# Two PSUM tiles in place of one, order edges at the context rows and key rotation, chain buffers turned by one, weight sums three steps later

## The chip, the cores and the metric

One Trainium2 chip, one core of it. The metric is the device time of one execution in microseconds, taken as the median of several runs. The engines are TensorE (PE, matmuls and transposes into PSUM), VectorE (DVE), ScalarE (ACT), GpSimd (POOL) and SyncE (SP); the last two mostly issue transfers (DMAs).

## The reference

One layer of a diffusion transformer block over 512 tokens of width 2048, with 256 context tokens. In float32:

```
h  = modulate(rmsnorm(x),   shift,   scale)          # from c @ w_ada
hc = modulate(rmsnorm(ctx), shift_c, scale_c)
kc, vc = keys and values of hc;  p = h @ w_in        # 2048 x 9216
q = rope(rmsnorm(q)) * d**-0.5 ;  k = rope(rmsnorm(k))
attn = softmax(q [k, kc]^T) [v, vc]                  # 12 query heads, 4 key/value heads of 128, 768 keys
y_a = (attn * silu(z_a)) @ w_proj_a
y_b = (fourier_mix(u_b) * silu(z_b)) @ w_proj_b
y   = (sigmoid(g_a) * y_a + sigmoid(g_b) * y_b) @ w_out
out = rmsnorm(x + gate * y) * final_g
```

## The kernel before

**Matmuls.** Every float32 factor is split in two halves, high and low (`split_from`, L174-177: ACT copies the high half, L176, and DVE subtracts it to get the low one, L177). `mm3` (L325-329) makes each product of three matmuls: high by high (L327), high by low (L328), low by high (L329). PSUM has eight banks of 512 float32 columns.

**Products of a group.** The large products are done in groups with seven products each (P1, Q5, P2, Q6, P7, Q3, Q4; a Strassen-like scheme), in place of eight. Each takes a form of the activations (A11, Z5, S2, S3, S4, A12, A22) by weights that are sums or differences of blocks. Groups 0 to 7 are the input projection (three of queries and gates, two of gates, group 5, `KV`, of keys and values together with the context's, two of gates); groups 10 and 11 are the projection of the attention branch; groups 8 and 9 the output projection. `Group.steps` runs the pieces of one product: `get` hands out the split weights of a piece, `mm` does its matmuls into an accumulator of two banks, and at a product's end DVE (L860) or ACT (L863, L868) empties the accumulator.

**The weight stream.** `stream_product` (L378) lists the pieces; `start_load` (L199) starts their loads on SP as buffers come free; `split_piece` splits them. Four of the seven weights are stages of a running sum in four chain buffers `chain[0..3]` (R in the profile), one for each piece: stage 0 is loaded, and after each split a POOL transfer adds the next block to the buffer (L280). `left[pc]` is 1 while a chain buffer is in use; a stage 0 isn't loaded before it is 0. `last_split` holds the instructions of the last split; `tc.issue_after` adds an order edge, so that what is emitted in it is issued behind the instruction named.

**Who sets the order.** The program is written as one sequence. A framework puts each engine's instructions in an order of its own within the dependencies, and places the semaphore waits: an instruction that writes a tile waits for those that read it before, and the other way round. Engines run their queues in order.

**Context and keys.** `context_row` (L1070) scales rows of the context by a modulation (four multiplications on DVE, L1077), makes the forms in one buffer `cparts` and stores them (`cf_d`). `rotations` (L931, L935) folds the norm's gain into the rotary tables, once for queries and once, before product Q5 of group 5, for keys, after `load_rotations` has loaded them.

**Attention.** PSUM is one tile of eight banks, `whole_psum` (L1200-1202). `banks[0]` is its first six banks and `banks[1]` the last two. The six are cut into four stretches of 768 columns, `wide[0..3]`, one and a half banks each. The loop over 48 steps (L1425-1479, one for each head and block of 128 queries) emits in each step:

- `scores(i)`: six matmuls into one of wide[0..2] in turn; maximum on DVE (L1272); exponential and sum on ACT (L1274).
- `values`, each second step: 18 matmuls of 256 columns for the half before, and two transposes of gates, into the last bank (`b1`); read by ACT (L1315) and DVE (L1316).
- `turn(i-1)`: six transposes of the probabilities (L1290) into wide[3], split into `pth` (L176) and `ptl` (L177).
- `fill`: groups of three matmuls of the other branch's projection into bank 6 (`fill_acc`), emptied by DVE at L1238.
- three times in the whole loop `get_keys`: six transposes and a split for the next keys; eleven times `turn_queries` into `b1`.
- `weight_sum`: six sums of three weight blocks, by a load (L1415), an accumulating load (L1416) and a store (L1417) on POOL, at the steps 10 to 27.

**Behind the attention** `pair` hands out pairs of banks from the same `banks`: 0 to 5 as accumulators, 6 and 7 for the transposes of merged rows (`turn_merged`, L1404), which ACT copies out (L1408). `branch_done` multiplies an accumulator by its gate (L1388), `out_done` by a row of gates (L1615).

## Time and profile before

| what | us |
|---|---|
| median of 3 runs | 1311.36 |
| lowest and highest run | 1309.23, 1312.31 |
| the profiled execution | 1312.46 |
| its span (first to last instruction) | 1310.7 |

The profile's page names each engine's busy time and share of the span, and groups of instructions by line. A timeline row holds start, length, engine, line, operation, what it writes and reads, the shape and, in brackets, how long the engine stood idle before it and what ended that. A row of groups holds the count, the busy time and the mean of one in ns, then the idle time before them. A window's row holds the busy time of PE, its weight loads, DVE, ACT and POOL with the counts of instructions, then the granted clock of PE, the share of the DMA engines and GB/s. Matmuls are pipelined: the time from one start to the next is the cadence, and it is shorter than the length in the row.

### The profile page before, as it was taken

Reading aid. Unit: us, or ns where it says so; the run is one execution under the profiler, and the core shown is the slowest. Engines: PE = TensorE matmul, PEld = TensorE weight load, DVE = VectorE, ACT = ScalarE, POOL = GpSimd, SP = SyncE. Lnnn points to the kernel's source line nnn. Section 1 sums busy time; section 2 is a strip of 40 time slices with the busy share of each in tenths; the row PEclk is TensorE's granted clock in tenths of the full one; section 3 lists DMA queues with packets and bytes.
Section 4 is the critical chain, followed back from the end, with each engine's and each line's share of the span. In section 5 each row is a group of like instructions: output and inputs, shape, how many; then the busy total and the mean of one; then the engine's idle time right before and its main releaser. Section 6 shows DMA issues by size and latency. Waiting matters only on the chain.

```text
span 1310.7 us, 17551 instructions
## 1 busy us (share of the span) xinstructions
PE 1281.5 (98%) x6522; PEld 1046.7 (80%) x6522; DVE 995.5 (76%) x1295; ACT 685.8 (52%) x1079; POOL 183.3 (14%) x244
## 2 busy tenths in 40 slices
PE   6999999999999999999999999999999999999997
PEld 3577888888888887888888888888888888788885
DVE  5666899989688876757677766688898867787676
ACT  5222655555556544544254554666667646465554
POOL 0110011110202110011021020012100212221210
PEclk9999999999999999999999999999999999999999
DMA  9898487887899979986869888578852899998985
GB/s 381 330 374 349 177 244 188 240 249 244 213 291 263 260 245 276 297 215 175 262 210 285 273 212 260 195 228 264 270 163 81 236 253 246 242 205 231 219 204 171
DMA packets 103718, 318.54 MB, mean 243 GB/s; under 512 B 9808, under 2 KB 33104, under 8 KB 99280
## 3 DMA queue, kind: packets, MB, share of 16 engines
q0 software_dynamic: 30288, 123.75, 39.9%
q1 hardware_dynamic: 48720, 163.65, 35.2%
q10 hardware_dynamic: 24624, 30.02, 6.7%
q8 instruction: 51, 0.84, 0.2%
q14 instruction: 35, 0.29, 0.1%
HBM read 283.30 MB, written 34.09 MB: 242 GB/s over the span
## 4 chain that ended last, share of the span: by engine, by line
PE 73%; DMA 10%; DVE 9%; issue 3%; ACT 3%; SPq 0%; POOL 0%; ACTq 0%; DVEq 0%
PE banks L327 10%; PE banks L328 10%; PE banks L329 9%; PE x L329 6%; PE x L328 6%; PE x L327 6%; PE y L328 5%; PE y L329 5%; PE y L327 5%; DMA wr<-in_w_g 4%; DVE wlo L177 3%; PE pd L532 2%; PE banks L1290 2%; PE pb L327 2%; DVE s L177 2%
## 5 line engine op out<-in xcount | busy, mean ns | idle before, releaser
L176 ACT ACTIVATE whi<-R 128x1024 fp32r<-128x1024 f32 x138 | 145.4, 1060 | 131.6 <-PE banks L329 44.6
L177 DVE TENSOR_TENSOR wlo<-R,whi 128x1024 fp32r<-128x1024 f32 x138 | 167.7, 1222 | 55.3 <-ACT whi L176 53.0
L177 DVE TENSOR_TENSOR wlo<-wr,whi 128x1024 fp32r<-128x1024 f32 (+1 forms) x123 | 148.7, 1214 | 58.8 <-ACT whi L176 58.7
L176 ACT ACTIVATE whi<-wr 128x1024 fp32r<-128x1024 f32 (+1 forms) x123 | 128.9, 1053 | 119.3 <-PE y L329 36.6
L327 PE MATMUL banks<-whi,s 128*128 128x512 f32 x396 | 157.1, 397 | 2.1 <-DVE ev L860 1.5
L328 PE MATMUL banks<-wlo,s 128*128 128x512 f32 x396 | 155.2, 392 | 0.8 <-DVE wlo L177 0.8
L329 PE MATMUL banks<-whi,s 128*128 128x512 f32 x396 | 155.1, 392 | 0.0
L328 PE MATMUL x<-wlo,s 128*128 128x512 f32 x352 | 137.3, 390 | 2.9 <-DVE wlo L177 2.9
L327 PE MATMUL x<-whi,s 128*128 128x512 f32 x352 | 137.2, 390 | 0.0
L329 PE MATMUL x<-whi,s 128*128 128x512 f32 x352 | 137.0, 389 | 0.0
L328 PE MATMUL y<-wlo,s 128*128 128x512 f32 x316 | 123.1, 390 | 0.5 <-DVE wlo L177 0.5
L327 PE MATMUL y<-whi,s 128*128 128x512 f32 x316 | 123.0, 389 | 0.3 <-DVE cxe L1013 0.3
L329 PE MATMUL y<-whi,s 128*128 128x512 f32 x316 | 122.8, 389 | 0.0
L280 POOL DMA_DIRECT2D R<-in_w_g x64 | 56.0, 876 | 423.6 <-DVE wlo L177 241.1
L176 ACT ACTIVATE s<-wr 128x512 fp32r<-128x512 f32 (+2 forms) x93 | 60.7, 677 | 69.2 <-DMA wr<-cf_d 23.7
L327 PEld LDWEIGHTS banks<-whi,s 128*128 128x128 f32 x396 | 74.4, 188 | 17.9 <-ACT whi L176 2.2
L177 DVE TENSOR_TENSOR s<-wr,s 128x512 fp32r<-128x512 f32 (+2 forms) x93 | 67.0, 751 | 27.4 <-ACT s L176 26.6
L329 PEld LDWEIGHTS banks<-whi,s 128*128 128x128 f32 x396 | 74.4, 188 | 15.5
L328 PEld LDWEIGHTS banks<-wlo,s 128*128 128x128 f32 x396 | 74.5, 188 | 15.0 <-DVE wlo L177 1.2
L328 PEld LDWEIGHTS x<-wlo,s 128*128 128x128 f32 x352 | 66.1, 188 | 17.9 <-DVE wlo L177 4.2
L327 PEld LDWEIGHTS x<-whi,s 128*128 128x128 f32 x352 | 66.1, 188 | 13.7
L329 PEld LDWEIGHTS x<-whi,s 128*128 128x128 f32 x352 | 66.1, 188 | 13.6
(293 smaller groups left out, 2835.4 us busy)
## 6 DMA issues: line engine op xcount, KB each, us to landing
wr<-in_w_g SPq DMA_DIRECT2D x128, 512.0 KB, 5.2
R<-in_w_g POOLq DMA_DIRECT2D x64, 512.0 KB, 7.2
wa<-in_w_ss POOLq DMA_DIRECT2D x26, 1024.0 KB, 8.4
R<-in_w_g SPq DMA_DIRECT2D x32, 512.0 KB, 5.7
wr<-in_w_gate SPq DMA_DIRECT2D x32, 512.0 KB, 5.1
wr<-in_w_o SPq DMA_DIRECT2D x24, 512.0 KB, 7.7
R<-in_w_o POOLq DMA_DIRECT2D x24, 512.0 KB, 8.5
wr<-in_w_pab SPq DMA_DIRECT2D x20, 512.0 KB, 6.0
```

The costliest lines, as they stand in the source:

```text
L176: first = nc.scalar.activation(hi, src, ACT.Copy)
L177: return first, nc.vector.tensor_tensor(lo, src, hi.bitcast(F32), op=ALU.subtract)
L280: nc.gpsimd.dma_start(chain[e.pc], e.nxt, accum_op=ALU.add)
L327: nc.tensor.matmul(o, ah, bh, start=start, stop=False, skip_group_check=cont)
L328: nc.tensor.matmul(o, ah, bl, start=False, stop=False, skip_group_check=cont)
L329: nc.tensor.matmul(o, al, bh, start=False, stop=stop, skip_group_check=cont)
L532: last = nc.tensor.matmul(acc[32 * j : 32 * j + 32, :256], c2[:, 8 * h + k, :], w[:, k, :], start=n < 4, stop=n >= KK - 4)
L1290: nc.tensor.transpose(tp[:, k * P : (k + 1) * P], p[:, k * P : (k + 1) * P], ident)
```

## The change

Four parts.

1. The four multiplications of each context row, and the rotation of the key tables, get an order edge behind the low half of the last weight split that was emitted.
2. The PSUM of the attention and of all behind it becomes two tiles, `banks` of six banks and `more` of two.
3. Groups 11, 8 and 9 begin with chain buffer 3, 2 and 2 in place of 0. `left` blocks all four buffers at the attention's start, and frees the fourth at its end.
4. The weight sums go from the steps 10 to 27 to the steps 13 to 30.

The number of instructions is the same on every engine.

```diff
+CHAIN_FROM = {BRANCH_A + 1: 3, 8: 2, 9: 2}
...
         for pc in range(pieces):
             key = (name, g, pc)
+            r = (pc + CHAIN_FROM.get(g, 0)) % 4
             if isinstance(what, tuple) and name == "P7" and g >= BRANCH_A:
-                stream(key, [p7_d[g - BRANCH_A, pc]], 1024, 2, pc=pc)
+                stream(key, [p7_d[g - BRANCH_A, pc]], 1024, 2, pc=r)
...
     def context_row(i, raw):
-        t, raw = cparts, raw.rearrange("p (b s c) -> p b s c", b=4, s=2)
+        t, raw, line = cparts, raw.rearrange("p (b s c) -> p b s c", b=4, s=2), last_split[-1][1].ins
...
-                nc.vector.scalar_tensor_tensor(t[:, 2 * q : 2 * q + 2, j, :], raw[:, 2 * q + j], gain[:, kb, 1:2],
-                                               crs.rearrange("p (s c) -> p s c", s=2), op0=ALU.mult, op1=ALU.mult)
+                with tc.issue_after(line):
+                    nc.vector.scalar_tensor_tensor(t[:, 2 * q : 2 * q + 2, j, :], raw[:, 2 * q + j], gain[:, kb, 1:2],
+                                                   crs.rearrange("p (s c) -> p s c", s=2), op0=ALU.mult, op1=ALU.mult)
...
             elif (g, name) == (KV, "Q5"):
-                rotations(1.0)
+                with tc.issue_after(last_split[-1][1].ins):
+                    rotations(1.0)
...
     psq = ctx.enter_context(tc.tile_pool(name="psq", bufs=1, space=PSUM, reuse_waits="tile"))
-    whole_psum = psq.tile([P, 8, 512], F32, name="banks")
-    banks += [whole_psum[:, :6, :], whole_psum[:, 6:, :]]
+    banks += [psq.tile([P, 6, 512], F32, name="banks"), psq.tile([P, 2, 512], F32, name="more")]
...
-    left[:3] = [1] * 3
+    left[:] = [1] * 4
...
-        if 10 <= i < 28:
-            n, step = divmod(i - 10, 3)
+        if 13 <= i < 31:
+            n, step = divmod(i - 13, 3)
...
     ats_.close()
+    left[3] = 0
```

The other two calls of `stream` in `stream_product` take `pc=r` in the place of `pc=pc` in the same way. Line numbers of the changed kernel are one to four higher than those of the kernel before.

More of the change, by code (lines that the diff above doesn't have):

```diff
@@ L384, in stream_product @@
             part = lambda i: w[CHAIN[i][0], CHAIN[i][1], pc]
+            r = (pc + CHAIN_FROM.get(g, 0)) % 4
             if isinstance(what, tuple) and name == "P7" and g >= BRANCH_A:
-                stream(key, [p7_d[g - BRANCH_A, pc]], 1024, 2, pc=pc)
+                stream(key, [p7_d[g - BRANCH_A, pc]], 1024, 2, pc=r)
             elif isinstance(what, tuple):
                 off = name == "P7"
-                stream(key, [w[a, b, pc] for a, b in what], 1024, 2, pc=pc, nxt=part(3) if off else None, off=off)
+                stream(key, [w[a, b, pc] for a, b in what], 1024, 2, pc=r, nxt=part(3) if off else None, off=off)
             else:
-                stream(key, [part(what)] if what in by_dve else [], 1024, 2, stage=what, pc=pc,
+                stream(key, [part(what)] if what in by_dve else [], 1024, 2, stage=what, pc=r,
                        nxt=part(what + 1) if what < (3 if g >= BRANCH_A else 2) and what + 1 not in by_dve else None)
```

## Prediction

> **What bounds the kernel now.** I read the page first, then the table of windows, then the timeline around each place where PE sits idle.

> ```profile
> span 1310.7 us, 17551 instructions
> ...
> PE 1281.5 (98%) x6522; PEld 1046.7 (80%) x6522; DVE 995.5 (76%) x1295; ACT 685.8 (52%) x1079; POOL 183.3 (14%) x244
> ```

> ```profile
> 828.00:1017.00 189.00, 187.23 (x1252) 164.25 (x1251) 157.08 (x256) 127.93 (x250) 25.25 (x41) 1.00 0.62 194
> 1030.00:1231.00 201.00, 199.69 (x915) 164.89 (x914) 153.69 (x136) 108.97 (x119) 42.52 (x53) 1.00 0.95 239
> ```

> PE is busy 1281.5 of 1310.7 us. The columns of the windows are length, busy PE, PEld, DVE, ACT, POOL, then the granted clock. PE is busy 187.23 of 189.00 us in the attention and 199.69 of 201.00 us in the stage behind it, at clock 1.00. So the matmul queue bounds both stages, and an edit pays only by taking away one of PE's few pauses; it costs whenever it makes PE wait. The pauses that the diff touches are these:

> ```profile
> 503.61 1.28 DVE L1077 SCALAR_TENSOR_TENSOR qr<-wr,gain,qr 128x256 f32<-128x256 f32 x3 [6.52 <-DMA cf_d<-qr]
> 506.33 0.50 PE L328 MATMUL x<-wlo,s 128*128 128x512 f32 x1 [0.62 <-DVE wlo L177]
> 519.89 1.29 DVE L935 SCALAR_TENSOR_TENSOR qr<-qr 128x512 f32<-128x512 f32 x2 [2.04 <-DMA qr<-in_qkg]
> 522.38 0.50 PE L328 MATMUL x<-wlo,s 128*128 128x512 f32 x1 [2.13 <-DVE wlo L177]
> ...
> 822.65 0.39 PE L329 MATMUL x<-whi,s 128*128 128x512 f32 x1
> ...
> 824.69 0.39 PE L329 MATMUL x<-whi,s 128*128 128x512 f32 x1
> 825.12 1.29 DVE L860 TENSOR_TENSOR ev<-x,ev 128x512 f32<-128x512 f32 x2 [0.40 <-PE x L329]
> 826.55 0.47 PE L327 MATMUL banks<-whi,s 128*128 128x512 f32 x1 [1.47 <-DVE ev L860]
> ...
> 1145.33 0.50 PE L328 MATMUL banks<-wlo,s 128*128 128x512 f32 x1 [0.75 <-DVE wlo L177]
> ```

> Twice DVE stands before a context row or the key rotation until a transfer lands, and the low half of a weight split stands behind it; PE loses 0.62 and 2.13 us. At the start of the attention PE waits for the last group's evacuation. A matmul of 512 columns starts every 0.227 us (822.65 to 824.69 in nine steps), so 824.69 to 826.55 holds 1.63 us of pause. At 1145 a weight chain is late by 0.75. Together that is 5.1 us, the most that the change can win at places it touches.

> **Part 1, order edges at the context rows and the key rotation.** Nothing is added or taken away; the four multiplications of each row and both of the rotation go behind the split that is queued at that point. Gain: 0.62 + 2.13 = 2.75. Late next are the row's forms, whose store feeds the context product some products later, and the rotated keys; DVE has 24% of the span free to make that up. Bounds: -2.75 and, if a form comes late by the same wait, +2. I take -2.75.

> **Part 2, PSUM as two tiles.** No instruction is added. But the waits change, as the built order of the changed kernel shows. With the one whole tile, a matmul waits only for readers of the banks that it writes. With `banks` and `more` apart, a writer of a tile waits for every earlier reader of that tile, whichever bank it read. In the attention this ties three of PE's jobs to each other. The transposes of a turn (L1290) now wait in all 47 steps for the exponential (L1274) of the scores issued before them, where 24 did, and the next scores wait in 43 steps for the low split (L177, ptl) of that turn, where 15 did. Each step becomes a chain without overlap: scores, maximum, exponential, turn, high split, low split, next scores. Its links, from rows:

> ```profile
> 828.01 0.28 PE L327 MATMUL banks<-s,s 128*128 128x256 f32 x1
> 828.13 0.28 PE L328 MATMUL banks<-s,s 128*128 128x256 f32 x1
> ...
> 829.27 0.96 DVE L1272 TENSOR_REDUCE gain<-banks 128x1 f32<-128x768 f32 x1 [1.74 <-PE banks L329]
> 830.27 0.91 ACT L1274 ACTIVATE s<-banks,gain 128x768 f32<-128x768 f32 x1 [1.07 <-DVE gain L1272]
> 831.07 0.20 ACT L1274 ACTIVATION_READ_ACCUMULATOR s<-banks,gain 128x1 f32 x1
> ...
> 837.07 0.82 PE L1290 MATMUL banks<-ident,s 128*128 128x128 f32 x6
> 837.92 0.81 ACT L176 ACTIVATE pth<-banks 128x768 fp32r<-128x768 f32 x1 [0.23 <-PE banks L1290]
> ...
> 846.81 0.81 ACT L176 ACTIVATE pth<-banks 128x768 fp32r<-128x768 f32 x1
> 847.65 0.96 DVE L177 TENSOR_TENSOR ptl<-banks,pth 128x768 fp32r<-128x768 f32 x1
> ...
> 864.17 0.95 DVE L177 TENSOR_TENSOR ptl<-banks,pth 128x768 fp32r<-128x768 f32 x1
> 865.17 0.88 PE L1290 MATMUL banks<-ident,s 128*128 128x128 f32 x6 [0.40 <-DVE ptl L177]
> ...
> 1016.20 0.28 PE L327 MATMUL banks<-s,s 128*128 128x256 f32 x1
> ```

> - first matmul of the scores to the maximum: 828.01 to 829.27, 1.26
> - maximum to exponential: 829.27 to 830.27, 1.00
> - exponential to its accumulator's end, 830.27 to 831.27, and about 0.05 until PE starts: 1.05
> - first transpose to the high split: 837.07 to 837.92, 0.85
> - high split to low split: 846.81 to 847.65, 0.84
> - low split to the next matmul of PE that waited for it: 864.17 to 865.17, 1.00

> Sum: 6.00 us a step. That each link keeps its length, the groups of the attention bear out: the mean is close to the row used.

> ```profile
> L1272 DVE TENSOR_REDUCE gain<-banks 128x1 f32<-128x768 f32 x48 | 45.4, 953 | 10.2 <-PE banks L329 9.6
> L177 DVE TENSOR_TENSOR ptl<-banks,pth 128x768 fp32r<-128x768 f32 x47 | 44.8, 954 | 10.8 <-ACT pth L176 10.4
> L1274 ACT ACTIVATE s<-banks,gain 128x768 f32<-128x768 f32 x48 | 43.3, 902 | 23.2 <-DVE gain L1272 22.8 <-DVE s L177 0.4
> ...
> L176 ACT ACTIVATE pth<-banks 128x768 fp32r<-128x768 f32 x47 | 38.2, 813 | 12.4 <-PE banks L1290 12.1
> ```

> Before, the first scores start at 828.01 and those of the 48th step at 1016.20: 188.2 us for 47 steps, 4.00 each. The chain at 6.00 is 2.00 longer, so 47 x 2.00 = **+94**. Before, the 2.00 were covered by PE doing the scores of one step while ACT and DVE worked on another; that cover is gone, and only fill groups (bank 6) and value products (bank 7) may run beside the chain.

> What doesn't fit comes on top. Three times new keys are transposed into `banks` and split: 0.85 + 0.84 + 1.00 = 2.7 each, **+8**. Between scores and turn the chain leaves PE 3.3 us from the first score's matmul (1.26 + 1.00 + 1.05). Every second step puts the scores (1.04), a fill's three matmuls (0.68) and a value product there (18 matmuls of 256 columns, one started 0.12 us after the other as at 828.01 and 828.13, and two transposes): about 4. Some of it now waits too, as bank 7 is in a tile with bank 6. Bounds for this: nothing, where all of it runs in the gaps behind the turn, and 24 x 0.7 = 17, where each such step is lengthened; I take half, **+8**. The other DVE and ACT work fits: 157.08 - 45.4 - 44.8 = 67 us on DVE is 1.4 a step, beside the 4.1 that the chain leaves it free, and ACT has less. Behind the last scores two turns end one after the other, and the first product of the next stage writes the same tile: 0 to +6, I take **+4**.

> At the attention's start the first fill goes to `more`, on which nothing waits: **-1.5** of the 1.63.

> Behind the attention the accumulators of the products are pairs of `banks`. Before, the next product writes another pair while DVE or ACT empties the last. Now its first matmul waits for that reader; I count 14 such new waits in the built order, 12 behind DVE and 2 behind ACT, and one that waits for a whole copy instead of a half.

> ```profile
> L860 DVE TENSOR_TENSOR s<-banks,s 128x1024 f32<-128x1024 f32 x7 | 8.6, 1223 | 1.7 <-PE banks L329 1.6
> ...
> L868 ACT COPY s<-banks 128x1024 f32<-128x1024 f32 x3 | 3.0, 1016 | 5.0 <-PE banks L329 5.0
> L1415 POOL DMA_DIRECT2D s<-in_w_pab x6 | 3.5, 588 | 5.5 <-ACT s L176 4.2 <-PE banks L329 1.0 <-issue 0.2
> ```

> The row at 825.12 shows the price: the reader starts 0.43 behind the start of the last matmul, and PE starts 0.14 behind the reader's end. With 1.22 in the middle, less the 0.23 of the cadence, that is 1.56; with 1.016 it is 1.36. So 12 x 1.56 + 2 x 1.36 = 21.4 and 0.5 for the half copy. In six of them eight transposes to `more` lie between and use 8 x 0.11 = 0.87 each: -5.2. **+17**; bounds 0 (all covered) and 26 (readers queued behind splits of 1.22 in a quarter of the cases).

> **Part 3, chain buffers turned by one.** The same loads, accumulations and splits, in other buffers, so that a group's first piece takes a buffer that came free earlier. It can take away the 0.75 at 1145 and what follows from it there: -1.3, bounds -1.7 and +1.3. With PE waiting more, transfers have more slack, and this gain is partly gone; I take **-1**.

> **Part 4, weight sums three steps later.** Six sums of three POOL DMAs each go three steps further back in POOL's queue, past loads of queries and gates; one issue takes 588 ns in the row above. They have some twenty steps until the branch product reads them. Nothing, bounds -0.5 and +1.

> **Sum.** The profiled execution took 1312.46 us, 1.1 above the median of the runs, 1.8 above its own span. 1312.5 - 2.75 + 94 + 8 + 8 + 4 - 1.5 + 17 - 1 = **1438**.

> **Rivals.** A measurement of this kernel resolves about 0.2%, 2.6 us.

> *Not slower: only the wait at the attention's start goes.* Place: the loop of scores and turns. If the tiles' waits are satisfied before PE reaches the instruction, PE's own work sets the step, 4.00 us. It decides where the chain takes 4.00 or less instead of 6.00, and the readers behind the attention end within the transposes. Then the time is 1312.5 - 2.75 - 1.5 - 1 = 1307. For it: 24 and 15 of such waits existed, and PE was idle for only 1.77 us of the attention's window. Against it: those left a step free between two links; now no step is left free.

> *Half the loop overlaps.* If the scheduler's order lets every second step hide its chain, 24 x 2.0 = 48 in the place of 94: 1392.

> *DVE's order.* If one op of 1.22 us stands ahead of a chain's link in every step, 47 x 1.22 = 57 in the place of the 8: 1487. Against it: 4.1 us free a step for 1.4 of work.

> *The clock falls.* PE would be busy 4 of each 6 us.

> ```profile
> 0.00:25.00 25.00, 14.51 (x68) 7.23 (x69) 12.74 (x29) 15.56 (x27) 1.90 (x11) 1.00 0.93 370
> ```

> In this window PE was busy 58% of the time, and the granted clock was 1.00; that speaks against it. At half the clock the scores' matmuls add 1.04 and the transposes 0.65 to each step: 47 x 1.7 = 80, and the time is 1518. [...]

> **How the numbers follow.** The forecast 0.82; not slower 0.05; half overlapped 0.05; DVE's order 0.04; the clock 0.04. The forecast's own terms reach from 1438 - 17 - 8 - 8 = 1405 (nothing behind the attention, the gaps take all, keys hidden) to 1438 + 9 + 9 + 2 + 17 = 1475 (readers queued, every second step lengthened, end dearer, and 0.36 us more a step). The others lie outside with 0.18 together, so the range is 1405 to 1475. Faster by over 0.2%: 0.04; within: 0.01; slower: 0.95.

> **What would show it.** In the changed profile the attention's window (first to 48th scores) is about 298 us long with PE some 65% busy; the transposes of the turn (now L1293) show idle released by the exponential (now L1277) and the scores (L328) idle released by the low split L178, about 1 to 2 us each, 47 times; behind it, first matmuls of products wait 1 to 1.6 us for L862, L870, L890 and L1391. The pauses at 506, 522 and 826 are gone. If PE is still over 95% busy in the attention, the tile-wide wait was not what I take it for, and the forecast falls; if the clock there is under 1.00, the fourth rival holds.

## The result, and the profile after

The changed kernel takes 1491.06 us (median of 6 runs, 1485.19 to 1503.48), the kernel before 1312.71 in the runs beside it. The ratio is 1.1379, with a 95% interval of 1.1324 to 1.1433: some 180 us slower. The forecast was 1438, the range 1405 to 1475; the sign was right, the size too small. The profiled execution took 1503.48 us, the longest of the six.

PE's busy share in 40 slices on the page of the kernel before, then the page of the changed kernel with its granted clock:

```profile
PE   6999999999999999999999999999999999999997
```

```profile
span 1501.5 us, 17557 instructions
...
PE 1358.9 (90%) x6522; PEld 1093.1 (73%) x6522; DVE 1003.4 (67%) x1295; ACT 692.5 (46%) x1079; POOL 181.1 (12%) x244
...
PE   7999999999999999999999767777777888898997
...
PEclk9999999999999999999999887877788999999999
```

PE was busy in nine tenths of nearly every slice before; now the slices 23 to 31, the attention, stand at 6 and 7, and the granted clock is at 7 and 8 tenths of full speed there. The windows of the attention and of the stage behind it:

```profile
823.00:1165.00 342.00, 254.66 (x1253) 205.46 (x1252) 170.65 (x265) 138.48 (x255) 26.86 (x43) 0.83 0.37 114
1165.00:1501.50 336.50, 293.62 (x1288) 236.97 (x1286) 215.38 (x209) 154.64 (x190) 53.32 (x66) 0.96 0.77 189
```

The first and the last maximum of the scores cut the span in three. Before, the first is the row at 829.27 in the prediction; the others are these, of before and then of the changed kernel:

```profile
1016.75 0.96 DVE L1272 TENSOR_REDUCE gain<-banks 128x1 f32<-128x768 f32 x1 [0.39 <-PE banks L329]
```

```profile
823.05 0.96 DVE L1275 TENSOR_REDUCE gain<-banks 128x1 f32<-128x768 f32 x1 [0.34 <-PE banks L330]
...
1164.19 0.96 DVE L1275 TENSOR_REDUCE gain<-banks 128x1 f32<-128x768 f32 x1 [1.06 <-PE banks L330]
```

| part of the span | before | after | difference | forecast |
|---|---|---|---|---|
| to the first maximum | 829.3 | 823.1 | -6.2 | -4.3 |
| first to 48th maximum | 187.5 | 341.1 | +153.7 | +110 |
| behind it, to the span's end | 293.9 | 337.3 | +43.4 | +20 |

So the places are those of the forecast, and two terms are short: 44 us in the attention and 23 behind it. What PE waited for in the attention, before (829 to 1017) and after (823 to 1165), as sum, times and longest wait:

```profile
PE banks L1129 <- DVE ptl L177: 0.8, 1, 0.8
PE banks L1290 <- DVE ptl L177: 0.4, 1, 0.4
PE banks L327 <- ACT s L1274: 0.4, 1, 0.4
```

```profile
PE banks L328 <- DVE ptl L178: 44.0, 42, 2.9
PE banks L1293 <- ACT s L1277: 21.1, 17, 2.1
PE more L328 <- ACT pth L177: 9.9, 11, 0.9
PE banks L1132 <- DVE ptl L178: 5.5, 3, 1.8
...
```

The two new waits are there by name: the scores (L328) behind the low split of the turn, 42 times, and the turn (L1293) behind the exponential. The turn shows only 17 of its 47: in the other steps PE had other work until the exponential ended, or longer.

### The profile page after: what moved, and what is told of

The parts are those of the page before. It is cut to its first block, busy times and chain, and to the rows that moved or that the text cites. A ratio compares the mean times of both kernels' runs of the same rounds, so it can differ in the third digit from the quotient of the medians.

```text
span 1501.5 us, 17557 instructions
## 1 busy us (share of the span) xinstructions
PE 1358.9 (90%) x6522; PEld 1093.1 (73%) x6522; DVE 1003.4 (67%) x1295; ACT 692.5 (46%) x1079; POOL 181.1 (12%) x244
## 4 chain that ended last, share of the span: by engine, by line
PE 77%; DVE 8%; DMA 6%; ACT 5%; issue 3%; POOL 0%; SPq 0%; ACTq 0%; POOLq 0%; DVEq 0%
PE x L330 7%; PE x L328 7%; PE x L329 7%; PE banks L328 6%; PE y L329 6%; PE y L328 6%; PE y L330 6%; PE banks L330 5%; PE banks L329 5%; DVE ptl L178 3%; PE more L328 3%; PE more L329 3%; PE more L330 3%; PE banks L1293 2%; DMA s<-yb_d 2%
## 5 line engine op out<-in xcount | busy, mean ns | idle before, releaser
L177 ACT ACTIVATE whi<-R 128x1024 fp32r<-128x1024 f32 x138 | 145.2, 1058 | 161.0 <-PE banks L330 78.0
L178 DVE TENSOR_TENSOR wlo<-R,whi 128x1024 fp32r<-128x1024 f32 x138 | 167.5, 1220 | 74.8 <-ACT whi L177 74.6
L178 DVE TENSOR_TENSOR wlo<-wr,whi 128x1024 fp32r<-128x1024 f32 (+1 forms) x123 | 148.4, 1212 | 89.7 <-ACT whi L177 87.0
L177 ACT ACTIVATE whi<-wr 128x1024 fp32r<-128x1024 f32 (+1 forms) x123 | 128.6, 1050 | 145.3 <-PE banks L330 41.1
L328 PE MATMUL banks<-whi,s 128*128 128x512 f32 x296 | 120.7, 408 | 25.6 <-DVE s L862 15.8
L328 PE MATMUL x<-whi,s 128*128 128x512 f32 x352 | 137.1, 390 | 0.0
L329 PE MATMUL x<-wlo,s 128*128 128x512 f32 x352 | 137.0, 389 | 0.0
L328 PE MATMUL y<-whi,s 128*128 128x512 f32 x316 | 123.0, 389 | 0.3 <-DVE cxe L1015 0.3
L329 PE MATMUL y<-wlo,s 128*128 128x512 f32 x316 | 123.0, 389 | 0.2 <-DVE wlo L178 0.2
L330 PE MATMUL banks<-whi,s 128*128 128x512 f32 x296 | 118.2, 399 | 0.0
L329 PE MATMUL banks<-wlo,s 128*128 128x512 f32 x296 | 118.1, 399 | 0.0
L328 PE MATMUL banks<-s,s 128*128 128x512 f32 (+1 forms) x144 | 63.7, 443 | 45.6 <-DVE ptl L178 44.0
L1277 ACT ACTIVATE s<-banks,gain 128x768 f32<-128x768 f32 x48 | 43.3, 902 | 132.5 <-DVE gain L1275 132.4
L178 DVE TENSOR_TENSOR ptl<-banks,pth 128x768 fp32r<-128x768 f32 x48 | 45.9, 957 | 69.6 <-ACT pth L177 69.5
L177 ACT ACTIVATE s<-wr 128x512 fp32r<-128x512 f32 (+2 forms) x93 | 60.4, 676 | 68.0 <-DMA wr<-cf_d 21.9
L178 DVE TENSOR_TENSOR s<-wr,s 128x512 fp32r<-128x512 f32 (+2 forms) x93 | 66.6, 748 | 34.6 <-ACT s L177 32.4
L328 PEld LDWEIGHTS banks<-whi,s 128*128 128x128 f32 x296 | 57.4, 194 | 42.5 <-ACT whi L177 15.0
L1275 DVE TENSOR_REDUCE gain<-banks 128x1 f32<-128x768 f32 x48 | 45.9, 957 | 57.7 <-PE banks L330 57.7
L328 PEld LDWEIGHTS banks<-s,s 128*128 128x128 f32 x144 | 31.5, 219 | 62.3 <-DVE ptl L178 55.4
```

The lines of the kernel that those rows point to most:

```text
L177: first = nc.scalar.activation(hi, src, ACT.Copy)
L178: return first, nc.vector.tensor_tensor(lo, src, hi.bitcast(F32), op=ALU.subtract)
L328: nc.tensor.matmul(o, ah, bh, start=start, stop=False, skip_group_check=cont)
L329: nc.tensor.matmul(o, ah, bl, start=False, stop=False, skip_group_check=cont)
L330: nc.tensor.matmul(o, al, bh, start=False, stop=stop, skip_group_check=cont)
L1275: maxima[0] = nc.vector.tensor_reduce(mx[:, 0:1], sc[:, :NKEY], axis=AX.X, op=ALU.max, negate=True)
```

## The experiments

**1. The two tiles alone.** The kernel before, with this edit only:

```diff
-    whole_psum = psq.tile([P, 8, 512], F32, name="banks")
-    banks += [whole_psum[:, :6, :], whole_psum[:, 6:, :]]
+    banks += [psq.tile([P, 6, 512], F32, name="banks"), psq.tile([P, 2, 512], F32, name="more")]
```

> The kernel before with nothing but its PSUM tile made two (six banks and two). Theory: the two tiles alone make the loss, because every writer of a tile waits for every earlier reader of it; the time is then that of the changed kernel, 1491 us, plus the about 4 us that the order edges and the chain buffers win: 1486 to 1502. Rival: a part of the loss comes from the other three parts (chain buffers blocked longer, weight sums later): 1330 to 1470. If the time is under 1330, the two tiles are not the cause.

Measured: 1499.98 us, ratio 1.140 (1.1358 to 1.1442). The window of the attention is as in the changed kernel:

```profile
827.00:1168.00 341.00, 253.68 (x1249) 204.57 (x1248) 169.84 (x264) 137.79 (x254) 26.84 (x43) 0.83 0.38 114
```

That is inside the expectation: the two tiles alone make the loss.

**2. All the rest without them.** The changed kernel with the first edit taken back.

> The changed kernel with one PSUM tile of eight banks again; the order edges, the chain buffers and the later weight sums stay. Theory: 1312.7 - 2.75 (two pauses of PE at 506 and 522) - 1 (the pause at 1145) = 1309, between 1306 and 1311, with the pause of 1.5 at the attention's start still there. Rival: the other parts cost too, now hidden under the pauses of the changed kernel: over 1313.

Measured: 1306.9 us, ratio 0.9952 (0.9938 to 0.9966), faster than before by about 6 us, a little more than expected. With the order edges alone (experiment 6, 1307.71) it is the fastest version of this study; the two can't be told apart. PE's longest wait from 490 us to the end is the one at the attention's start, which stays:

```profile
PE banks L328 <- DVE ev L862: 1.5, 1, 1.5
...
```

**3. and 4. Is it the clock?** Extra matmuls between scores and turn and behind the turn, at the places of the changed kernel where PE waits; they add work and nothing to the output.

```diff
+    def busy(i, n):
+        h, t = divmod(i, 4)
+        kh = kv[h // GQ][0]
+        for k in range(n):
+            nc.tensor.matmul(b1()[:, 256:512], kh[:, :P], kh[:, :256], start=i < 4, stop=True, skip_group_check=True)
...
+        if i < NSTEP and (i % 2 or i < 4):
+            busy(i, 10)
...
             turn(i - 1)
             divide(i - 1)
+            busy(min(i, NSTEP - 1), 10)
```

> The changed kernel with 740 matmuls more in the attention, of 256 columns each, whose result is overwritten unread; they stand between scores and turn and behind the turn, where PE waits. They need 740 x 0.118 = 87 us of PE at full clock. [...] With PE kept busy the clock stays at 1.00 in the attention, the window from the first to the 48th maximum goes from 341 to between 290 and 315 us, and the time from 1491 to between 1440 and 1470, though PE has more to do. Rival: the halved clock falls into pauses and costs nothing, the links of the chain are longer for other reasons; then the time stays at 1491 or grows by up to 40 us.

The second run has `busy(..., 5)` in both places.

> The changed kernel with 370 matmuls more in the attention whose result is overwritten unread, half as many as in the run before, at the same places. [...] With half the extra work most windows stay above that: under 40 us at half clock in the attention (119 in the changed kernel, 0 with 740 matmuls), the window of 48 maxima between 305 and 320 us. If it is under 315, the 740 matmuls cost something in the chain themselves, and the clock's price is more than the 26 us read so far. Rival: the clock goes with the extra work in proportion: 60 us at half clock and 328 us.

Measured: 1477.23 us with 740 matmuls more, 1476.95 with 370. The windows from the first to the 48th maximum, of the run with 740 and of the run with 370:

```profile
824.00:1139.00 315.00, 286.41 (x1963) 252.08 (x1963) 169.16 (x262) 136.03 (x253) 24.85 (x40) 1.00 0.40 119
```

```profile
824.00:1135.00 311.00, 253.99 (x1611) 217.04 (x1611) 169.14 (x264) 138.63 (x254) 26.85 (x43) 0.97 0.41 124
```

More work for PE, less time: the window falls from 342 to 315 and to 311 us. In the records of the granted clock of the changed kernel 119 us of this window are at half speed, with 370 matmuls more 20 us, with 740 none. So 99 us less at half speed go with 30 us less time (341 - 311): 0.3 for each microsecond. My estimate for a PE that is always busy is half of it, from the scores' matmuls, which take 2.09 us at half speed (882.58 to 884.67) and 1.07 at full (828.01 to 829.08 in the kernel before).

The extra matmuls could have a price of their own, so here are the steps one by one, each from the first matmul of its scores to that of the next. Of the 47 steps, 14 ran at full speed both in the changed kernel and with 370 matmuls more: 86.6 us together in the one, 86.8 in the other. In 25 steps the changed kernel was at half speed for 90 us in sum and the other run not at all: 194.9 and 166.0 us, 0.32 for each microsecond at half speed. So the halved clock costs the attention of the changed kernel some 35 to 38 us (118 us between the first and the last maximum, at 0.30 to 0.32).

The first run's rival is out. Its time stayed above the expected 1470 because that took the window's gain off the median of 1491, while the window of 341 us is that of the profiled execution, 1503; 26 us less is 1477. In the second run the expectation is met, and its rival, a clock in proportion to the extra work, is out. The second run's forecast has most windows above some busy share of PE, and no run shows such a share: in the changed kernel's trace stretches of 3.41 us with 0.26 to 0.56 came ahead of half speed, and others with 0.46 and more ahead of full speed (last section). In the run with 740, 31 of the extra matmuls waited for DVE, 19 us in sum; that may be why its window is 4 us longer than with half of them. The whole times of the two are the same.

**5. Another cut.** Four banks and four, two wide stretches and one single bank in each.

```diff
-            return banks[0][:, tag : tag + 2, :] if tag < 6 else banks[1]
+            return banks[tag // 4][:, tag % 4 : tag % 4 + 2, :]
...
-            return banks[0][:, b : b + 2, :] if b < 6 else banks[1]
+            return banks[b // 4][:, b % 4 : b % 4 + 2, :]
...
-    banks += [psq.tile([P, 6, 512], F32, name="banks"), psq.tile([P, 2, 512], F32, name="more")]
+    banks += [psq.tile([P, 4, 512], F32, name=n) for n in ("banks", "more")]
...
-    wide = [flat(banks[0])[:, NKEY * i : NKEY * i + NKEY] for i in range(4)]
-    fill_acc, b1 = banks[1][:, 0, :], lambda: banks[1][:, 1, :]
+    wide = [flat(banks[i // 2])[:, NKEY * (i % 2) : NKEY * (i % 2) + NKEY] for i in range(4)]
+    fill_acc, b1 = banks[0][:, 3, :], lambda: banks[1][:, 3, :]
```

> The changed kernel with its PSUM cut 4 + 4 instead of 6 + 2: two of the wide stretches and one single bank in each tile, the pairs 0 and 2 in one, 4 and 6 in the other. Theory: the loss goes with the number of stretches that share a tile. In the built order the transposes of a turn wait for an exponential 8 times instead of 47, the scores for the low split 12 times instead of 43, but the fills now wait for exponentials 32 times; a part of the serial chain is left: 1340 to 1420, with a mean clock between 0.97 and 1.00. Rival: any two tiles cost the same, as the fills and values now take part in the chain: 1480 or more.

Measured: 1474.91 us, ratio 1.1237 (1.1211 to 1.1263). My expectation is missed by 55 us, and the rival is nearer. The mean clock was 0.965 to 0.967 in the four runs, and 84 of the 320 us between the first and the last maximum were at half speed. PE's waits in the attention show why:

```profile
PE banks L328 <- ACT s L1277: 23.5, 16, 1.8
PE more L1293 <- DVE ptl L178: 16.1, 10, 2.2
PE more L1139 <- DVE ptl L178: 13.7, 8, 2.0
PE more L328 <- DVE ptl L178: 8.2, 7, 1.9
...
```

Other jobs wait now: a fill in bank 3 (L328 into `banks`) for an exponential that reads the banks beside it, the transposes of queries (L1139) for a low split. Counting only the waits of the two jobs that had waited in the other cut told nothing; in both cuts, whoever shares a tile with the scores takes part in their chain.

**6. to 8. The other three parts, each alone, on the kernel before.** The edits are those of the diff.

> The kernel before with the order edges at the context rows and the key rotation, and nothing else. Theory: the pauses at 506, 522 and 542 us go, 0.78 + 2.29 + 0.67 = 3.7 us of PE's cadence: 1309.8 to 1310.3 where before stands at 1313.6, a ratio near 0.997. Rival: the late forms of a context row hold back the context's product, and a pause of the same size comes there: ratio 0.999 to 1.001.

> The kernel before with the chain buffers turned by one and all four blocked during the attention, and nothing else. Theory: the pause of 1.3 us at 1145 goes and nothing comes in its place: ratio 0.999. Rival: the first load of the branch groups' buffers waits for the fourth buffer to be freed at the attention's end, and a pause comes there: ratio 1.000 to 1.002.

> The kernel before with the six weight sums three steps later, and nothing else. Theory: no engine waits for them before or after, ratio 1.000 within 0.001. Rival: the sums of the kernel before stand ahead of loads of queries in POOL's queue and cost pauses of about 0.4 to 0.8 us in the attention's first half; then the ratio is 0.999.

Measured: order edges 0.9953 (0.9937 to 0.9969); chain buffers 0.9992 (0.9979 to 1.0005); weight sums 1.0005 (0.9986 to 1.0024). With the edges DVE multiplies the row that stood 6.52 us before without a wait, all four together:

```profile
505.96 1.67 DVE L1078 SCALAR_TENSOR_TENSOR qr<-wr,gain,qr 128x256 f32<-128x256 f32 x4
```

The edges make the whole measurable gain, more than expected. For the chain buffers the time can't be told from no change, but in that run's trace PE's wait of 0.8 at 1145 is gone. The weight sums do nothing that can be measured; the 0.999 of their rival is inside the interval.

**9. and 10. The stage behind the attention by itself.** Both kernels have one tile in the attention, close its pool behind the loop and begin the branch's first product there instead of in the loop's last steps. The first then takes two tiles, the second one tile again.

```diff
-    psq = ctx.enter_context(tc.tile_pool(name="psq", bufs=1, space=PSUM, reuse_waits="tile"))
-    banks += [psq.tile([P, 6, 512], F32, name="banks"), psq.tile([P, 2, 512], F32, name="more")]
+    psqs, psq = region("psq", None, space=PSUM, reuse_waits="tile")
+    whole_psum = psq.tile([P, 8, 512], F32, name="banks")
+    banks += [whole_psum[:, :6, :], whole_psum[:, 6:, :]]
...
-        if i == NSTEP - 1:
-            a_groups.append(a_group(0))
-            first = a_groups[0].steps("P1")
-        if NSTEP > i - 2 >= NSTEP - 3:
-            next(first)
-            next(first)
     ats_.close()
+    psqs.close()
+    psr = ctx.enter_context(tc.tile_pool(name="psr", bufs=1, space=PSUM, reuse_waits="tile"))
+    banks[:] = [psr.tile([P, 6, 512], F32, name="banks"), psr.tile([P, 2, 512], F32, name="more")]
+    a_groups.append(a_group(0))
+    first = a_groups[0].steps("P1")
```

> One PSUM tile in the attention, and two tiles (six banks and two) for all that comes behind it; the first product of the branch, which had begun in the last three steps of the loop, begins behind the loop, so the attention's end is bare. To be read against the run beside it, which is the same with one tile behind too. Theory: the stage behind the attention loses by its own waits what the changed kernel's trace shows there, pauses of PE of 32 us in sum less the 3 of before, and some more by the halved clock: 27 to 42 us over the run beside it. Rival: my sum of 17 was right, and the rest of the 43 us came from the attention's delay (late transfers, a clock that is down already): 14 to 20 us.

> One PSUM tile in the attention and one again, newly allocated, behind it; the first product of the branch begins behind the loop. It is the base for the run beside it. Theory: against the changed kernel with one tile throughout (1307) it loses only the cover at the attention's end, the first product's 2 to 10 us, and no wait between products: 1308 to 1320.

Measured: 1356.47 and 1317.22 us, 39 apart, both as expected. PE's waits behind the attention with two tiles, and with one:

```profile
PE banks L328 <- DVE s L862: 15.8, 7, 4.8
PE more L1408 <- DMA s<-yb_d: 5.7, 2, 4.5
PE banks L328 <- DVE s L1392: 3.0, 2, 1.6
...
```

```profile
PE banks L328 <- ACT pth L177: 1.8, 2, 0.9
PE banks L1294 <- ACT s L1278: 1.6, 1, 1.6
PE banks L328 <- ACT s L865: 1.6, 3, 1.2
...
```

All waits of PE behind the last maximum add up to 39.0 us with two tiles and 7.9 with one, so 31 of the 39 us are waits. Of the other 8 a part may be the clock, as 23 us there are at half speed with two tiles and 14 with one; it was not measured apart. The waits of this stage are its own, not a consequence of the late attention, and my 17 was about half of their price.

## Why the prediction was right and wrong

Two steps failed: that the clock stays, a term of nothing in the sum that cost some 35 to 38 us in the attention, and the term behind the attention, 17 us that measured 39. The chain of waits in the attention was right to some 7 us.

**What bounds the kernel, and that PE's waits cost:** right. The two tiles were picked out as the part that decides, with its mechanism and its places, and experiments 1 and 2 show that.

**Part 1**, -2.75: the measured ratio gives -4.1 to -8.3 us. Direction and place were right, and the term was small, as it was read from one execution. In the profile of the chain buffers alone, which has the same two pauses, they take 0.76 + 3.33 = 4.1 us:

```profile
506.74 0.50 PE L329 MATMUL x<-wlo,s 128*128 128x512 f32 x1 [0.76 <-DVE wlo L178]
523.98 0.50 PE L329 MATMUL x<-wlo,s 128*128 128x512 f32 x1 [3.33 <-DVE wlo L178]
```

They end on a transfer's landing, and that moves from run to run: 0.62 and 2.13 in the kernel before, 0.57 and 2.92 with the weight sums alone. The third pause that I named for the run with the edges alone stayed, with 0.32 us at 540.

**Part 2, the chain**, 6.00 us a step. Each link, as the mean of 46 steps from the starts of its instructions:

| link | forecast | changed kernel | with 740 matmuls more, full clock |
|---|---|---|---|
| scores to maximum | 1.26 | 1.78 | 1.36 |
| maximum to exponential | 1.00 | 1.05 | 1.07 |
| exponential to turn | 1.05 | 1.31 | 1.21 |
| turn to high split | 0.85 | 0.98 | 0.95 |
| high to low split | 0.84 | 0.87 | 0.87 |
| low split to next scores | 1.00 | 1.30 | 1.28 |
| sum | 6.00 | 7.29 | 6.75 |

The last link holds the three key loads; its median is 1.01. The links on ACT and DVE keep the length that they have in the rows of before. The links with matmuls in them, scores, turn and the value products ahead of the turn, grew. In the changed kernel's own trace, 15 of these 46 steps ran wholly at full clock; they took 6.30 us each, close to the 6.00. The 11 that spent more than half of their time at half clock took 8.23. With the extras (+8 keys, +8 for what doesn't fit) the forecast for the window was 298 us. With 370 matmuls more it is 311, of which 20 us at half clock cost some 6; so at full clock the sum was some 7 us short.

**The step that failed in the attention is "The clock falls".** I left it out of the sum, gave it 0.04 and argued from a window of 25 us in which PE was busy 58% at clock 1.00. Cut finer, that row says nothing of the kind: PE did nothing in the first 6.8 us and was busy without a break from 11.6 to 18.4.

```profile
0.00:3.41 3.41, 0.00 (x0) 0.00 (x0) 0.90 (x6) 1.51 (x2) 1.90 (x11) 1.00 0.38 90
3.41:6.80 3.39, 0.00 (x0) 0.00 (x0) 0.00 (x0) 1.55 (x2) 0.00 (x0) 1.00 1.02 393
...
11.60:15.00 3.40, 3.40 (x9) 1.34 (x8) 3.28 (x6) 2.76 (x5) 0.00 (x0) 1.00 1.05 434
15.00:18.40 3.40, 3.40 (x23) 1.28 (x21) 0.85 (x2) 1.38 (x4) 0.00 (x0) 1.00 0.98 406
```

```profile
875.16:878.57 3.41, 2.03 (x9) 1.40 (x9) 2.66 (x4) 1.23 (x2) 0.00 (x0) 1.00 0.00 0
878.57:881.99 3.42, 1.25 (x7) 0.82 (x7) 2.93 (x6) 2.41 (x5) 1.07 (x2) 1.00 0.44 150
881.99:885.40 3.41, 2.82 (x10) 2.53 (x11) 1.03 (x2) 0.00 (x0) 0.00 (x0) 0.50 0.93 329
885.40:888.82 3.42, 3.42 (x18) 3.42 (x18) 0.63 (x2) 1.40 (x3) 1.03 (x2) 0.50 0.73 277
888.82:892.23 3.41, 1.57 (x14) 1.33 (x13) 1.78 (x3) 1.07 (x2) 0.91 (x2) 1.00 0.76 115
```

```profile
882.58 0.58 PE L328 MATMUL banks<-s,s 128*128 128x256 f32 x1 [0.61 <-DVE ptl L178]
...
883.39 0.63 PE L328 MATMUL banks<-s,s 128*128 128x512 f32 x1
883.82 0.63 PE L329 MATMUL banks<-s,s 128*128 128x512 f32 x1
884.24 0.63 PE L330 MATMUL banks<-s,s 128*128 128x512 f32 x1
884.67 0.41 PE L329 MATMUL more<-ptl,s 128*128 128x256 f32 x1
```

PE was busy 1.25 of 3.42 us; in the next stretch the clock is 0.50, and the scores take 882.58 to 884.67, 2.09 in the place of the 1.04 that I had reckoned for full speed. Behind a stretch with PE busy for 3.42 of 3.42 us it is back at 1.00. No wait in the attention was longer than 2.9 us, and still 119 us of it ran at half speed. My price for the rival, all of the attention at half clock, was too high (80; some 35 to 38 measured), and the chance far too low.

**Part 2, behind the attention**, 17, bounds 0 to 26. Measured: 39 (experiments 9 and 10). The single waits came out as priced: several are 1.57 from cadence to cadence, where I had 1.56. What was missed are two other forms. After product Q6 (L862) DVE makes three subtractions one after the other, and the last one still reads an accumulator in `banks`:

```profile
1219.41 1.23 DVE L178 TENSOR_TENSOR wlo<-wr,whi 128x1024 fp32r<-128x1024 f32 x1 [1.50 <-ACT whi L177]
1221.04 1.22 DVE L862 TENSOR_TENSOR s<-banks,s 128x1024 f32<-128x1024 f32 x1 [0.40 <-PE banks L330]
1222.18 1.21 DVE L178 TENSOR_TENSOR wlo<-wr,whi 128x1024 fp32r<-128x1024 f32 x1
1223.31 1.22 DVE L862 TENSOR_TENSOR s<-s,s 128x1024 f32<-128x1024 f32 x1
1224.45 1.21 DVE L862 TENSOR_TENSOR s<-s,banks 128x1024 f32<-128x1024 f32 x1
```

```profile
1225.80 0.77 PE L328 MATMUL banks<-whi,s 128*128 128x512 f32 x1 [4.80 <-DVE s L862]
```

PE stood 4.80 us, twice in the stage (1226 and 1304), where I had counted one reader of 1.22. And the transposes of merged rows, due a fixed number of pieces later, now came to PE before the transfer that they need had landed: 5.7 us. In the changed kernel 27 us behind the last maximum ran at half clock too, 5 before.

**The attention's start**, -1.5: the wait for the last evacuation is gone from the changed kernel's trace, and it is there in experiment 2, where the tile is one. But 0.78 us come back at once, as a fill waits for the evacuation of the fill before it:

```profile
825.16 0.50 PE L328 MATMUL more<-whi,s 128*128 128x512 f32 x1 [0.78 <-DVE R L1241]
```

**Parts 3 and 4**, -1 and nothing: neither can be told from no change, as said.

The forecast's sum was 1438 for a run that measured 1491, or 1503 in the profiled execution. The runs of the changed kernel differ by 18 us, and they go with the clock: 1485.19 at a mean of 0.972, 1503.48 at 0.952. By estimate from these means, with the two speeds of the records, that is some 60 us more at half speed (2 x 0.020 x 1500), and again 0.3 for each.

## What to carry to other kernels

A tile is also a unit of waiting: before one PSUM tile is cut or joined, compare the waits of the built program on both sides, for every job that writes any of the tiles. A chain of waits that lets PE stand for a quarter of the time cost twice here (254.66 of 342 us busy, 119 us at half speed), once as a chain and once in the clock, so price both; whether a clock's row speaks for a kernel with pauses is read from windows as short as the clock's own records (3.41 us here), never from a mean. Where a reader follows a product, count every instruction up to the last one that reads the tile.

## What the runs showed that I had not expected

- The clock's price is bought back by useless work: 740 matmuls more, some 87 us of PE at full clock, made the changed kernel 14 us faster, and 370 did the same.
- In the attention of the changed kernel, the stretches of 3.41 us at full speed go like this (busy time by the rows' lengths): 23 in which PE was busy for 0.26 to 0.56 of the time were followed by half speed, 42 with 0.46 and more by full speed. So between 0.46 and 0.56 the share alone doesn't decide. Of those at half speed, 22 with 0.82 and more were followed by full speed, 12 with 0.62 to 0.83 by half speed again.
- With one tile of eight banks a matmul waits for readers of its banks; with 6 + 2 and with 4 + 4 it waits for readers of banks beside them. Why the program's waits come out so differently was not settled.
